# The RWKV stage of a bidirectional diffusion step: A of both directions first, block transfers on two queues, one stationary for the output side

## The chip, the core and the metric

The kernel runs on one core of a Trainium2 chip. The metric is the device time of one execution in microseconds (us), the median of several executions. The engines of the core that matter are the TensorE (PE in the profile: matmuls; PEld is its loading of stationary operands), the VectorE (DVE), the ScalarE (ACT), GpSimd (POOL) and the SyncE (SP), which here does nothing but issue DMAs. Each engine works through its instructions in the order of the program and waits at an instruction until what it needs is there; so a waiting instruction holds everything behind it on its engine, also the DMAs that are issued from that engine's queue.

## The reference

One step of a hybrid block over 640 tokens of width 2048 (512 latent tokens and 128 context tokens): a projection into eight parts, an RWKV-7 scan in both directions over 16 heads of 64 channels, an RG-LRU branch, a gated merge, and an output projection.

```python
def rwkv7_scan(r, w, k, v, kk, a, s0, reverse):
    def step(s, inp):
        r_t, w_t, k_t, v_t, kk_t, a_t = inp
        s_kk = jnp.einsum('bhvk,bhk->bhv', s, kk_t)
        s = s * w_t[:, :, None, :] - s_kk[..., None] * (kk_t * a_t)[:, :, None, :] + v_t[..., None] * k_t[:, :, None, :]
        return s, jnp.einsum('bhvk,bhk->bhv', s, r_t)
...
    z = xm @ p['w_in']
    r, k, v, g_a, x_b, g_b, m_a, m_b = jnp.split(z, SPLITS, axis=-1)
    r = r + (shift_fn(r) - r) * mu[0]
...
    for d in range(2):
        dirs_a.append(rwkv_direction(...))
```

The shift averages a token's neighbours: four on the grid for the latent tokens, two for the context tokens.

## The kernel before

**The background of matmuls.** All large products go through `product`, which runs over the K tiles of a product in steps (`piece`, L318): each step is six PE matmuls of 128x320 (L331). After each step `tick` (L229) lets the side work advance by one `yield`. So the program is one long row of steps, called **ticks** here, between which the side work's instructions are placed; how many ticks lie between two pieces of side work is written out in tuples (W, INV, QI, X1 and so on, L46 to L53). For every second tick one part of the next weights is split into a high half by ScalarE (`wh`, L313) and a low half by GpSimd (`wl`, L314), five parts (ten ticks) ahead of its use, into five buffers. Raw weights come by SP's queue (L301) into three buffers.

**The RWKV stage.** It goes over eight groups i of two heads (128 channels). Beside group i run seven products (`hosts`), 112 ticks; the first has nine and the seventh eight. Three generators work side by side: `mixed` shifts the r, k and v of group i+1 (`mix`, L755); `normed` (L885) prepares its decays and keys (`over` writes bk, the two key sides, L846); `rwkv` (L938) does the scan of group i in chunks of 64 tokens, ten chunks (NC) in two directions d and two heads e; then `norm` (L1219) closes group i.

**One scan, in ticks from its start.** `decayed` (L858) multiplies -kk and r by their decays into one tile st4. `first` (L951) multiplies each chunk's 64x64 key block with both halves of st4 (128 columns): its first half, masked, is A (`ats`), its second the r side (`rbs`). Six calls, three for each direction, ticks 2 to 14. `send` (L997) stores A's 32x32 diagonal blocks in DRAM; from there they come back with one block in a row (xn at L1069, xi at L1088), ScalarE turns them (L1092, L1095), and from tick 24 on VectorE inverts 80 triangular blocks at once by 30 steps of two operations (L1100, L1102). Between these steps lie `second` (L969: the other key side, again 128 columns, with VectorE's L982 bringing it in) and `turned` (L987: the keys transposed, `toks`). At tick 48 VectorE's copy L1109 has the inverses in both orders, four stores (L1113) take them to DRAM, at tick 53 four loads (tf, L1121) and eight loads (qm, L1127) bring them back; at tick 60 PE multiplies them with A's off-diagonal blocks (L1136, L1150) to get the inverse of the whole 64x64 block. From tick 64 on eight serial steps s (L1163) run through the chunks: `px` (L1169) and one half of the output `py` (L1173), a copy by ScalarE (L1176), `pu` (L1181), `put` into the tile sv (L1028 on ScalarE, L1029 on VectorE), then `pn` (L1190), the other half of `py` (L1194), and the new state (L1198, L1200). They end at tick 105. `ps1` gives one of four PSUM tiles in turn.

## Time and profile before

| | us |
|---|---|
| median of 3 executions | 2215.8 (2215.31 to 2216.61) |
| the profiled execution, its own time | 2214.5 |
| its span, first to last instruction | 2212.7 |
| scan of one group, from one L1136 to the next | 150.5 to 151.3 |
| one tick (six matmuls of L331) | 0.88 |

The granted TensorE clock is 0.981 on average. The profile gives busy times by engine, the waits with what ended them, and a timeline in which several equal instructions are merged into one row (start, length, engine, line, operation, shapes, count, and in brackets the idle time before it). A matmul's length in it overlaps the next one's; what a matmul costs is the distance of the starts.

### The profile page before, as it was taken

The page shows a single profiled execution, that of the slowest core. Times are in us where ns is not written, and L with a number is a line of the kernel's source. Part 1 is how long each engine was busy: PE and PEld are TensorE (multiplying, and loading weights), DVE is VectorE, ACT ScalarE, POOL GpSimd, SP SyncE. Part 2 cuts the span into 40 slices and gives each one's busy share as a digit, 9 for nine tenths or more (in the row PEclk, how much of TensorE's full clock was granted, in tenths as well). Part 3 has the DMA queues.
Part 4 walks back from the last instruction along what each step waited for, and adds up shares of the span by engine and source line. Part 5 has one row for each costly group of instructions (what it writes and reads, how often), then busy time and mean ns, then how long its engine had stood idle before and what let it go on. Part 6 is the DMA issues. An engine that isn't in the chain of part 4 may idle for free.

```text
span 2212.7 us, 47527 instructions
## 1 busy us (share of the span) xinstructions
PE 2106.8 (95%) x18248; PEld 1960.3 (89%) x18248; DVE 1371.9 (62%) x2661; ACT 973.4 (44%) x2262; POOL 882.9 (40%) x1167
## 2 busy tenths in 40 slices
PE   6999999999998998998989989989999899999997
PEld 3789999998888898898888988989989799999997
DVE  4755765687746756676676467665632699733354
ACT  3346776643443444434434434444333422234554
POOL 2244554553333333333333333334323465543343
PEclk9999999999999999999999999999999999999999
DMA  9953334332323222223223222232322767544474
GB/s 368 343 160 129 129 107 132 100 98 82 92 73 89 70 81 87 74 77 96 59 83 92 80 85 71 79 89 82 85 86 85 251 225 223 183 148 156 150 242 153
DMA packets 203507, 281.64 MB, mean 127 GB/s; under 512 B 69360, under 2 KB 91056, under 8 KB 202768
## 3 DMA queue, kind: packets, MB, share of 16 engines
q1 hardware_dynamic: 202832, 277.38, 39.8%
q8 instruction: 144, 2.36, 0.4%
q0 software_dynamic: 448, 1.23, 0.2%
q14 instruction: 83, 0.68, 0.1%
HBM read 237.70 MB, written 39.85 MB: 125 GB/s over the span
## 4 chain that ended last, share of the span: by engine, by line
PE 73%; DVE 16%; DMA 5%; issue 3%; ACT 1%; SPq 1%; POOL 0%; ACTq 0%; DVEq 0%; POOLq 0%
PE pj L331 55%; PE rw L591 3%; DVE tmp L1100 2%; DVE junk L1349 2%; DVE xi L1102 2%; PE rw L958 2%; PE rw L499 2%; DVE gws L1351 1%; PE pj L499 1%; PE rw L976 1%; PE rw L1181 1%; DVE st L982 1%; PE rw L1169 1%; DMA wr<-ws 1%; PE ada L385 1%
## 5 line engine op out<-in xcount | busy, mean ns | idle before, releaser
L314 POOL TENSOR_TENSOR wl<-wr,wh 128x256 fp32r<-128x256 f32 x922 | 792.5, 868 | 1230.1 <-ACT wh L313 1177.2
L331 PE MATMUL pj<-xh,wh 128*128 128x320 f32 (+2 forms) x2976 | 761.1, 323 | 1.4 <-ACT wh L313 1.4
L331 PE MATMUL pj<-xh,wl 128*128 128x320 f32 (+2 forms) x2976 | 724.8, 311 | 1.7 <-DVE wl L314 1.5
L331 PE MATMUL pj<-xl,wh 128*128 128x320 f32 (+2 forms) x2976 | 723.5, 310 | 0.0
L313 ACT ACTIVATE wh<-wr 128x256 fp32r<-128x256 f32 x1048 | 421.5, 413 | 512.4 <-PE pj L331 394.0
L331 PEld LDWEIGHTS pj<-xh,wh 128*128 128x128 f32 x2976 | 502.5, 190 | 33.6 <-issue 14.4
L331 PEld LDWEIGHTS pj<-xh,wl 128*128 128x128 f32 x2976 | 511.9, 189 | 4.1 <-DVE wl L314 2.5
L331 PEld LDWEIGHTS pj<-xl,wh 128*128 128x128 f32 x2976 | 512.8, 189 | 0.1
L1100 DVE TENSOR_TENSOR tmp<-xn,xi 104x30 f32<-104x30 f32 (+14 forms) x240 | 100.4, 418 | 81.0 <-ACT xn L1095 74.5
L1029 DVE COPY sv<-rw 64x128 f32<-64x128 f32 x80 | 23.6, 295 | 198.5 <-ACT sv L1028 197.3
L314 DVE TENSOR_TENSOR wl<-wr,wh 128x256 fp32r<-128x256 f32 x126 | 57.6, 458 | 127.2 <-ACT wh L313 127.1
L1102 DVE TENSOR_TENSOR xi<-xi,tmp 104x30 f32<-104x30 f32 (+14 forms) x240 | 98.7, 411 | 8.2
L1349 DVE SCALAR_TENSOR_TENSOR junk<-gws,cb 128x512 f32<-128x512 f32 x64 | 67.6, 1056 | 9.7 <-ACT cb L1341 9.7
L331 PE MATMUL pj<-yah,wh 128*128 128x320 f32 x256 | 59.3, 313 | 7.6 <-ACT g L1262 7.6
L982 DVE TENSOR_TENSOR st<-rw,c 64x512 f32<-64x512 f32 (+1 forms) x96 | 57.6, 600 | 12.4 <-PE rw L976 10.2
L1351 DVE SCALAR_TENSOR_TENSOR gws<-gws,cb 128x512 f32<-128x512 f32 x64 | 61.4, 959 | 1.9
L331 PE MATMUL pj<-yah,wl 128*128 128x320 f32 x256 | 59.3, 313 | 0.6 <-POOL wl L314 0.6
L331 PE MATMUL pj<-ybh,wh 128*128 128x320 f32 x256 | 58.6, 310 | 0.6 <-DVE thx L1385 0.4
L331 PE MATMUL pj<-yal,wh 128*128 128x320 f32 x256 | 59.1, 313 | 0.0
L331 PE MATMUL pj<-ybh,wl 128*128 128x320 f32 x256 | 58.6, 310 | 0.3 <-POOL wl L314 0.3
L331 PE MATMUL pj<-ybl,wh 128*128 128x320 f32 x256 | 58.3, 309 | 0.0
L1028 ACT ACTIVATE sv<-rw 64x128 f32<-64x128 f32 x80 | 21.7, 271 | 74.7 <-PE rw L1181 69.0
(776 smaller groups left out, 3088.0 us busy)
## 6 DMA issues: line engine op xcount, KB each, us to landing
wr<-w_in SPq DMA_DIRECT2D x312, 256.0 KB
adaw<-ada_w SPq DMA_DIRECT2D x64, 512.0 KB
wr<-w_o SPq DMA_DIRECT2D x128, 256.0 KB
gws<-ada_g SPq DMA_DIRECT2D x64, 256.0 KB
thl<-th SPq DMA_DIRECT2D x32, 320.0 KB
th<-thl SPq DMA_DIRECT2D x32, 320.0 KB
thm<-g SPq DMA_DIRECT2D x64, 160.0 KB
thx<-thm SPq DMA_DIRECT2D x32, 320.0 KB
```

The lines of the kernel that those rows point to most:

```text
L313: S.activation(h, r, AF.Copy)
L314: lows[pos[1] % len(lows)].tensor_tensor(lo, r, h.bitcast(F32), ALU.subtract)
L331: PE.matmul(p[:, :t1 - t0], w, x[:, t0:t1], start=(k == 0 and a == 0), stop=(k == nk - 1 and a == 2))
L499: PE.matmul(p[:, :HT], u[:, w], x[:, t], start=new, stop=end)
L591: PE.matmul(p, a, b, start=(n == 0), stop=(n == 2))
L958: PE.matmul(pa[hd(e), x:x + P], z.bk[d][hd(e), n, e], st4s[d][hd(e), n, e].rearrange("p a t -> p (a t)"), start=True, stop=True)
L982: V.tensor_tensor(st4s[d][so, n0:n0 + nn, e], pb[so, :m].rearrange("p (c a t) -> p c a t", a=2, t=CH), mb[so], ALU.mult)
L1029: V.tensor_copy(sv[hd(1), a, 1], src[hd(1), b])
L1100: V.tensor_tensor(t, xn[:NV, j, j + 1:].unsqueeze(2).to_broadcast([NV, m, j]), xi[:NV, j, :j].unsqueeze(1).to_broadcast([NV, m, j]), ALU.mult)
L1102: V.tensor_tensor(xi[:NV, j + 1:, :j], xi[:NV, j + 1:, :j], t, ALU.add)
L1349: V.scalar_tensor_tensor(junk, w, 1.0, cbs[h][:, 0], ALU.mult, ALU.mult, accum_out=gs[:, h, n, 0:1])
L1351: V.scalar_tensor_tensor(w, w, 1.0, cbs[h][:, 1], ALU.mult, ALU.mult, accum_out=gs[:, h, n, 1:2])
```

## The change

A of both directions now comes first. The r side is taken out of `first` and `second`: `decayed` is split into `inward` (-kk by its decay, into the tiles `sts`) and an `outward` of the scan's preparation (r by its decay, `z.rp`, done at the end of `normed`). `first` and `second` (now `across`) multiply 64 columns instead of 128, in two calls of five chunks for a direction instead of three. The r side is made by the new `outward(d, n0)`: both key sides together are one stationary operand of 64x128, so that one matmul gives both halves (`ros`). In the serial steps the output `py` comes after `pn` in one go: sv with `ros`, then the state `sc_` with `z.rp`. A lies in the bytes of `toks`, so `turned` moves behind the inverse, to ticks 63 and 64. Values and the bonus move behind `first`.

A of the backward direction goes to DRAM by ScalarE's queue, as do two of the four stores of the inverses and the four loads of `blocks(1)`, three ticks after the rest. VectorE, not ScalarE, turns the backward blocks. The tuples of ticks are new: the inverse starts at tick 15 and has 33 ticks (it was 24 and 23), the stores are at tick 49, PE's use of the inverses at tick 59, the serial steps go from tick 65 to 104. `mix` adds the neighbours with six VectorE operations straight into r, k or v, without a tile for the sum. The slots are 14 instead of 13.

```diff
-QB, NQ, HP, BC, BG = 21, 7, (4, 3, 3), 5, 2
-W = (2, 2, 2, 2, 2, 2, 2, 2, 2, 1, 3, 2)
-INV = (0, 1, 1, 1, 1, 1, 1, 1, 2, 2, 2, 2, 2, 2, 2, 2)
-QI = (1, 5, 7, 3, 1)
-X1 = (1, 2, 1, 1, 2, 1, 1, 1)
-X2 = (2, 2, 2, 2, 2, 1, 2, 2)
+QB, NQ, HP, BC, BG = 20, 6, (4, 3, 3), 4, 2
+LQA = 3
+W, SD, LD = (2, 1, 4), 0, (4, 6)
+MV, MX = (1, 2, 2), 3
+IW = (1, 3, 5, 7, 9)
+INV = (0, 1, 1, 2, 2, 3, 2, 3, 3, 2, 3, 3, 2, 2, 2, 2)
+QI = (1, 2, 8, 3, 1, 0, 1)
+X1 = (1, 2, 1, 1, 2, 0, 1, 1)
+X2 = (3, 2, 2, 1, 2, 1, 2, 1)
...
+NSLOT = 14
...
-                s = slot("sh")
-                sv = chunks(s)
-                V.tensor_tensor(sv[:, 0:8], zr[:, :, 0:64], zr[:, :, 2:66], ALU.add)
...
-                V.scalar_tensor_tensor(o[:, :TS], s[:, :TS], dc(3 + q, i), o[:, :TS], ALU.mult, ALU.add)
-                V.scalar_tensor_tensor(o[:, TS:T], s[:, TS:T], dc(6 + q, i), o[:, TS:T], ALU.mult, ALU.add)
+                ov, m4, m2 = chunks(o), dc(3 + q, i), dc(6 + q, i)
+                for x, y in ((ov[:, 0:8], zr[:, :, 0:64]), (ov[:, 0:8], zr[:, :, 2:66]), (ov[:, 1:8], zr[:, 0:7, 1:65]),
+                             (ov[:, 0:7], zr[:, 1:8, 1:65])):
+                    V.scalar_tensor_tensor(x, y, m4, x, ALU.mult, ALU.add)
+                    yield
+                for y in (zp[:, 0:128], zp[:, 2:130]):
+                    V.scalar_tensor_tensor(o[:, TS:T], y, m2, o[:, TS:T], ALU.mult, ALU.add)
...
+            def outward(self, d):
+
+                t = self.r if d else slot("rp")
+                V.tensor_tensor(chunks(t), chunks(self.r), self.pin[d], ALU.mult)
+                self.rp[d] = chunks(t)
...
+            def inward(self, d, st):
+
                 for e in range(2):
-                    sl = hd(e)
-                    V.tensor_tensor(self.st4[d][sl, n, e, 0], chunks(self.nk)[sl, n], self.pex[d][sl, n], ALU.mult)
-                    V.tensor_tensor(self.st4[d][sl, n, e, 1], chunks(self.r)[sl, n], self.pin[d][sl, n], ALU.mult)
+                    V.tensor_tensor(st[hd(e), :, e], chunks(self.nk)[hd(e)], self.pex[d][hd(e)], ALU.mult)
...
+            for d in range(2):
+                yield
+                z.outward(d)
+            z.th = z.kd = z.pin = z.k = z.r = None
...
-            st4s = z.st4 = [rp.tile([P, NC, 2, 2, CH], F32, tag=f"st4{d}", name="st4") for d in range(2)]
-            rbs = [rp.tile([P, NC, CH], F32, tag=f"rb{d}", name="rb") for d in range(2)]
+            sts = [rp.tile([P, NC, 2, CH], F32, tag=f"st{d}", name="st") for d in range(2)]
+            ros = [rp.tile([P, NC, 2, CH], F32, tag=f"ro{d}", name="ro") for d in range(2)]
...
-            ats = [None, None]
+
+            ats = [t[:, :, 0] for t in toks]
...
             def first(d, n0):
 
-                nn = min(4, NC - n0)
-                pa, m = ps1(), nn * P
-                for n in range(n0, n0 + nn):
-                    x = P * (n - n0)
-                    for e in range(2):
-                        PE.matmul(pa[hd(e), x:x + P], z.bk[d][hd(e), n, e],
-                                  st4s[d][hd(e), n, e].rearrange("p a t -> p (a t)"), start=True, stop=True)
+                pa = ps1()
+                for n, e, x in both(n0):
+                    PE.matmul(pa[hd(e), x], z.bk[d][hd(e), n, e], sts[d][hd(e), n, e], start=True, stop=True)
 
                 def bring():
-                    mb = mask[d].unsqueeze(1).to_broadcast([P, nn, 2, CH])
-                    pav = pa[:, :m].rearrange("p (c a t) -> p c a t", a=2, t=CH)
-                    V.tensor_tensor(chunks(ats[d])[:, n0:n0 + nn], pav[:, :, 0], mb[:, :, 0], ALU.mult)
-                    V.tensor_tensor(rbs[d][:, n0:n0 + nn], pav[:, :, 1], mb[:, :, 1], ALU.mult)
+                    V.tensor_tensor(ats[d][:, n0:n0 + 5], five(pa), wide(mask[d][:, 0]), ALU.mult)
...
-            def second(d, n0):
...
-                    x = P * (n - n0)
-                    for e in range(2):
-                        PE.matmul(pb[hd(1 - e), x:x + P], z.bk[d][hd(e), n, 1 - e],
-                                  st4s[d][hd(e), n, e].rearrange("p a t -> p (a t)"), start=True, stop=True)
...
+            def across(d, n0):
+
+                pk = ps1()
+                for n, e, x in both(n0):
+                    PE.matmul(pk[hd(1 - e), x], z.bk[d][hd(e), n, 1 - e], sts[d][hd(e), n, e], start=True, stop=True)
+                for e in range(2):
                     so = hd(1 - e)
-                    V.tensor_tensor(st4s[d][so, n0:n0 + nn, e],
-                                    pb[so, :m].rearrange("p (c a t) -> p c a t", a=2, t=CH), mb[so], ALU.mult)
-
-                return lambda: bring(0), lambda: bring(1)
+                    V.tensor_tensor(sts[d][so, n0:n0 + 5, e], five(pk)[so], wide(mask[d][:, 0])[so], ALU.mult)
+
+            def outward(d, n0):
+
+                po = [ps1(), ps1()]
+                for n, e, x in both(n0):
+                    PE.matmul(po[e][:, x], z.bk[d][hd(e), n].rearrange("p a t -> p (a t)"), z.rp[d][hd(e), n],
+                              start=True, stop=True)
+                for e in range(2):
+                    V.tensor_tensor(ros[d][:, n0:n0 + 5, e], five(po[e]), wide(mask[d][:, 1]), ALU.mult)
...
                         p0 = CH * e + HB * b
-                        nc.sync.dma_start(sa[d][0][2 * e + b].rearrange("n r c -> r n c"),
-                                          chunks(ats[d])[p0:p0 + HB, :, HB * b:HB * (b + 1)])
+                        (nc.sync, nc.scalar)[d].dma_start(sa[d][0][2 * e + b].rearrange("n r c -> r n c"),
+                                          ats[d][p0:p0 + HB, :, HB * b:HB * (b + 1)])
...
-            z.decayed(0, 0, 4)
...
-            values(0)
-            yield from idle(W[0])
...
+            def moved():
+
+                values(0, 4)
+                values(4, 8)
+                yield
+                values(8, NC)
+
+                pb = heads([z.bonus])
+                for s in range(2):
+                    h = slice(s * HT, (s + 1) * HT)
+                    V.tensor_tensor(v[:, h], v[:, h], pb[s][:, :HT], ALU.mult)
+                z.bonus = None
+                yield
+                for f in (across, outward):
+                    for d in range(2):
+                        for n0 in (0, 5):
+                            f(d, n0)
+                            yield
+
+            for d in range(2):
+                z.inward(d, sts[d])
             yield from idle(W[2])
-            bring()
-            bring = first(0, 8)
...
+            for d in range(2):
+                bring = first(d, 0), first(d, 5)
+                for f in bring:
+                    f()
+                later(SD, lambda d=d: send(d))
+
+                later(LD[d], lambda x=(xn[0:NB], xi[64:NV])[d], d=d: nc.sync.dma_start(
+                    x, sa[d][0].rearrange("g n r c -> (g n) r c")))
+                yield from idle(W[d])
+            z.nk = z.pex = None
             work = moved()
+            for n in MV:
+                next(work)
+                yield from idle(n)
+            S.activation(xi[0:NB], xn[0:NB].rearrange("p j t -> p t j"), AF.Copy)
             next(work)
-            yield from idle(W[7])
...
-            S.activation(xn[64:NV], xi[64:NV].rearrange("p t j -> p j t"), AF.Copy)
-            yield from idle(W[11])
+            yield from idle(MX)
+            V.tensor_copy(xn[64:NV], xi[64:NV].rearrange("p t j -> p j t"))
...
                 if j % 2 == 0:
-                    next(work, None)
+                    if j // 2 in IW:
+                        next(work)
                     yield from idle(INV[j // 2])
-            for _ in work:
-                pass
             V.memset(xi[:NV].rearrange("p t s -> p (t s)")[:, ::HB + 1], 1.0)
             V.tensor_copy(xn[:NV], xi[:NV].rearrange("p t s -> p s t"))
             yield from idle(QI[0])
-            for d in range(2):
-                for w, x in ((1, xi), (2, xn)):
-                    nc.sync.dma_start(sa[d][w].rearrange("g n r c -> (g n) r c"), x[64 * d:64 * d + NB])
-            yield from idle(QI[1])
+            for w, x in ((1, xi), (2, xn)):
+                for d in range(2):
+                    (nc.sync, nc.scalar)[w - 1].dma_start(sa[d][w].rearrange("g n r c -> (g n) r c"),
+                                                          x[64 * d:64 * d + NB])
+            for _ in work:
+                yield from idle(QI[1])
...
-            for o in (1, 0):
+            def blocks(o):
...
-                        nc.sync.dma_start(qm[d][p0, :, HB * b:HB * (b + 1)],
-                                          sa[d][2 - d][2 * e + b].rearrange("n r c -> r n c"))
+                        (nc.sync, nc.scalar)[o].dma_start(qm[d][p0, :, HB * b:HB * (b + 1)],
+                                                          sa[d][2 - d][2 * e + b].rearrange("n r c -> r n c"))
+
+            blocks(0)
+            later(LQA, lambda: blocks(1))
             put(0, 4, sc_)
...
             yield from idle(QI[4])
+            for n in range(4):
+                turned(n % 2, n // 2 * 5)
+                yield from idle(QI[5 + n % 2])
...
-                px, py = ps1(), ps1()
-                for x in range(np_):
...
-                for x in range(np_):
-                    for e in range(2):
-                        PE.matmul(py[hd(e), x * CH:(x + 1) * CH], sv[:, at(s, x), e], st4s[x % 2][:, ch[x], e, 1],
-                                  start=(x == 0), stop=False, skip_group_check=True)
+                xe = [(x, e, slice(x * CH, (x + 1) * CH)) for x in range(np_) for e in range(2)]
+                px = ps1()
+                for x, e, o in xe:
+                    PE.matmul(px[hd(e), o], sts[x % 2][:, ch[x], e], sv[:, at(s, x), e], start=True, stop=True)
...
                 if s < 7:
                     pn = ps1()
...
-                for x in range(np_):
-                    for e in range(2):
-                        PE.matmul(py[hd(e), x * CH:(x + 1) * CH], sv[hd(e), at(s, x), e], rbs[x % 2][hd(e), ch[x]],
-                                  start=False, stop=True, skip_group_check=True)
+                    for x, e, o in xe:
+                        PE.matmul(pn[hd(e), o], toks[x % 2][:, ch[x], e], sv[:, at(s, x), e], start=True, stop=True)
+                py = ps1()
+                for x, e, o in xe:
+                    PE.matmul(py[hd(e), o], sv[:, at(s, x), e], ros[x % 2][:, ch[x], e], start=(x == 0), stop=False,
+                              skip_group_check=True)
+                for x, e, o in xe:
+                    PE.matmul(py[hd(e), o], sc_[hd(e), x], z.rp[x % 2][hd(e), ch[x]], start=False, stop=True,
+                              skip_group_check=True)
```

More of the change, by code (lines that the diff above doesn't have):

```diff
@@ L734, in slot @@
         def slot(name, dtype=F32):
[L735 removed]
+            return rp.tile([P, SLOT], dtype, tag="rs", name=name, bufs=NSLOT)
         def mixed(q, i):
@@ L1033, in rwkv @@
             G.memset(sc_[:, 2:4], 0.0)
-            values(0)
-            yield from idle(W[0])
-            values(1)
-            bring = first(0, 0)
-            z.decayed(0, 4)
-            yield from idle(W[1])
-            ats[0] = slot("at")
-            bring()
-            bring = first(0, 4)
-            z.decayed(1, 0, 4)
-            yield from idle(W[2])
-            bring()
-            bring = first(0, 8)
-            z.decayed(1, 4)
-            yield from idle(W[3])
-            bring()
@@ L1051, in rwkv @@
-            z.pin = z.pex = None
-            later(2, lambda: send(0))
-            bring = first(1, 0)
-            yield from idle(W[4])
-            ats[1] = slot("at")
-            bring()
-            bring = first(1, 4)
-            pb = heads([z.bonus])
-            yield from idle(W[5])
-            bring()
-            bring = first(1, 8)
-            yield from idle(W[6])
-            bring()
-            for s in range(2):
-                h = slice(s * HT, (s + 1) * HT)
-                V.tensor_tensor(v[:, h], v[:, h], pb[s][:, :HT], ALU.mult)
@@ L1068, in rwkv @@
-            later(2, lambda: send(1))
-            later(2, lambda: nc.sync.dma_start(xn[0:NB], sa[0][0].rearrange("g n r c -> (g n) r c")))
-            def moved():
-                for d in range(2):
-                    for n0 in (0, 4, 8):
-                        for bring in second(d, n0):
-                            yield
-                            bring()
-                        if n0 < 8:
-                            yield
-                            turned(d, n0 // 4 * 5)
-                        yield
+            def moved():
[14 more added lines that the diff above has]
+                            yield
@@ L1093, in rwkv @@
-            yield from idle(W[10])
-            next(work)
-            S.activation(xn[64:NV], xi[64:NV].rearrange("p t j -> p j t"), AF.Copy)
-            yield from idle(W[11])
+            yield from idle(MX)
+            V.tensor_copy(xn[64:NV], xi[64:NV].rearrange("p t j -> p j t"))
             for j in range(1, HB - 1):
```

79 lines of the change are left out of this document (24 added, 55 removed).

## Prediction

> **What bounds the kernel now.** First the page: the busy times, and the chain that ended last by engine.
>
> ```profile
> PE 2106.8 (95%) x18248; PEld 1960.3 (89%) x18248; DVE 1371.9 (62%) x2661; ACT 973.4 (44%) x2262; POOL 882.9 (40%) x1167
> PE 73%; DVE 16%; DMA 5%; issue 3%; ACT 1%; SPq 1%; POOL 0%; ACTq 0%; DVEq 0%; POOLq 0%
> ```
>
> PE has work for 95% of the span, so a change pays where it takes matmuls away or ends a wait of PE. The change touches only the RWKV stage. Next, PE's waits there, from 440 to 1760 us (us in all, times, longest), and PE's timeline around one of them:
>
> ```profile
> PE rw L1136 <- DMA xi<-scr: 39.0, 12, 6.3
> ```
> ```profile
> 1011.24 2.08 PE L1136 MATMUL rw<-xi,at 32*32 32x32 f32 x80 [5.55 <-DMA xi<-scr]
> 1013.25 0.90 PE L331 MATMUL pj<-xh,wh 128*128 128x320 f32 x2
> ...
> 1016.45 0.45 PE L331 MATMUL pj<-xh,wh 128*128 128x320 f32 x2
> 1017.43 0.89 PE L1150 MATMUL rw<-qm,xn 32*32 32x32 f32 x80
> ```
>
> PE stands 39.0 us in all for the inverses to come back from DRAM, 5.55 us here. The price is higher than the gap, because PE runs slowly behind it: the 80 small matmuls of L1136 take 2.08 us and those of L1150 later 0.89, so 1.2 us are lost there; the twelve matmuls from 1013.25 to 1016.45, two ticks, take 3.20 us instead of 1.76, so 1.4 us more. One wait costs 5.55 + 2.6 us.
>
> Who is late? VectorE, in the inverse of the next group. PE's timeline, then VectorE's, and VectorE's work from 1118.4 to 1156.3 in groups by line (busy us, mean ns):
>
> ```profile
> 1115.39 1.09 PE L976 MATMUL rw<-st,bk 64*64 64x128 f32 x16
> ...
> 1162.33 0.74 PE L1136 MATMUL rw<-xi,at 32*32 32x32 f32 x6 [6.25 <-DMA xi<-scr]
> ```
> ```profile
> 1118.49 0.19 DVE L1100 TENSOR_TENSOR tmp<-xn,xi 104x30 f32<-104x30 f32 x1 [9.49 <-ACT xn L1095]
> ...
> 1155.15 1.09 DVE L1109 COPY xn<-xi 104x1024 f32<-104x1024 f32 x1
> ```
> ```profile
> L1100 DVE TENSOR_TENSOR tmp<-xn,xi 104x30 f32<-104x30 f32 (+14 forms) x30 | 13.2, 438 | 10.3 <-ACT xn L1095 9.5
> L1102 DVE TENSOR_TENSOR xi<-xi,tmp 104x30 f32<-104x30 f32 (+14 forms) x30 | 11.9, 397 | 1.0
> L982 DVE TENSOR_TENSOR st<-rw,c 64x512 f32<-64x512 f32 (+1 forms) x10 | 5.8, 582 | 0.3
> ```
>
> From the first step to the end of the copy (1155.15 + 1.09) VectorE needs 37.75 us: 25.1 for the inverse, 5.8 for L982, the rest the mixing of r, the copy and gaps. Another 6.1 us go by through DRAM until PE can start (1156.24 to 1162.33). PE meanwhile passes tick 24 at 1118.2 (1115.39, 1.0 for the 16 matmuls, two ticks) and stands at tick 60 at 1156.1 (1162.33 less 6.25): 37.9 us for 36 ticks. So 0.3 + 37.75 + 6.1 - 37.9 gives back the wait of 6.25 us.
>
> **The change part by part.** PE's own work first, by the distance of the starts:
>
> ```profile
> 1022.17 0.68 PE L1181 MATMUL rw<-xt__12636,qm 64*64 64x64 f32 x16
> 1022.78 0.56 PE L331 MATMUL pj<-xh,wh 128*128 128x320 f32 x2
> ...
> 1091.37 1.09 PE L958 MATMUL rw<-st,bk 64*64 64x128 f32 x16
> 1092.39 0.56 PE L331 MATMUL pj<-xh,wh 128*128 128x320 f32 x2
> ...
> 1094.35 0.65 PE L958 MATMUL rw<-st,bk 64*64 64x128 f32 x8
> 1094.93 0.56 PE L331 MATMUL pj<-xh,wh 128*128 128x320 f32 x2
> ...
> 1112.10 0.53 PE L992 MATMUL rw<-c,bk 64*128 64x64 f32 x10
> 1112.55 0.56 PE L331 MATMUL pj<-xh,wh 128*128 128x320 f32 x2
> ```
>
> Removed for each group: `first` and `second`, eight calls of 16 matmuls at 1.02 us and four of 8 at 0.58, 10.5 us. Added: `first` with 2 x 20 matmuls of the form of L1181 (0.61 for 16, so 0.038 each), 1.5 us; `across` with four calls of ten, 0.45 each, 1.8; `outward` with four calls of ten in the tile form of L992 (0.45), 1.8. That makes 5.1 us, and some 0.2 more because the ten transposes of the values fall into three calls. Saved: 5.2 us, over eight groups **42 us**. `outward` is a real product where L992 transposes, so its price is bounded: 0.038 a matmul as L1181, or 0.064 as the 128 column matmuls of L958, which would take back 0.7 us a group. I take 0.045, its own form. The serial steps keep their matmuls, and `turned` only moves.
>
> Now the wait. The new schedule gives from VectorE's turning copy (tick 15) to PE's use (tick 59) 44 ticks, 38.7 us, plus six calls at 0.45 and about 0.1 for changing over, 42.0 us: 4.1 more than the 37.9 of before, although PE's own work there shrank. VectorE's part: the turned copy is new on it (1.1 us, as the 1024 elements of L1109; bounded above by the 2.10 us that ScalarE takes for the same block, L1095 below); the ten L982 go (5.8) and four operations of `across` and six of `outward` come, of 320 elements each where L982 has 427 in the mean at 0.58 us: some 0.48, bounded above by 0.58, so 4.8 us. So 37.75 + 1.1 - 1.0 = 37.9 us. The six operations of `mix` handle as many elements as before; I cost them at nothing, and they lie in VectorE's row behind the inverse's steps, so an extra 0.3 us each would be 1.8 us more on the wait. Of the way through DRAM I expect 0.4 us less, since two of the four stores start on ScalarE's queue beside SP's (an issue takes some 0.46, by the row of L1001 below). The start counts like the 0.3 of before: A leaves at tick 7, backward blocks come at tick 12, and the load has three ticks and a call (3.1 us), which xn's load also had. Together 0.3 + 37.9 + 5.7 - 42.0 = 1.9 us of wait, bounded by 0 and, with a copy of 2.1 us, slower masked products (1 us) and slower mixing (1.8), by 6.
>
> What a short wait costs, besides itself, is read from two others in PE's timeline:
>
> ```profile
> 551.95 0.54 PE L882 MATMUL rw<-qhh,blk 128*128 128x320 f32 x1 [3.04 <-DVE st L982]
> ...
> 553.62 0.73 PE L331 MATMUL pj<-xl,wh 128*128 128x320 f32 x2
> ...
> 1052.49 0.45 PE L1169 MATMUL rw<-sv,st 128*64 128x64 f32 x8 [1.34 <-ACT sv L1028]
> ```
>
> After 3.04 us two matmuls of L331 are long (0.73; a pair at full rate has 0.45 in the row at 1016.45). After 1.34 us the eight small matmuls are not: 0.45, beside 0.68 for sixteen in the row of L1181. I let 1.9 us cost only itself: 8 x 1.9 = 15 us. The Trainium skill, "TensorE: Matmul & The Clock Gate", Part 1, has TensorE fall to half its clock after an idle window of about 3.4 us, free running; by that rule a wait of 1.9 us would as a rule stay free of the 2.6 us. The trace agrees on the half rate, and shows it after 3.04 us already.
>
> Away go the waits of before: 39.0, with 2.6 for each of the seven groups that show one, 18, and in the first group the 3.04 us above with some 2 of slow matmuls (PE waits there for a PSUM tile that a late L982 holds; `outward` frees its tiles long before): **62 us**.
>
> New waits. In the serial steps `py` no longer lies between `px` and `pu`; one step has no tick at all between them (X1[5] is 0), so PE waits for ScalarE's copy (bounded above by 0.39 us, half the row of L995 below, which has 320 elements instead of 128) and two handovers, some 0.7 us. ScalarE gets `turned`'s eight copies (0.77 a pair) right behind the copies of the inverse, before the first `pu`: 3.1 us of work in a place that was free of it; I put 1.2 us on PE. Ten DMAs are issued from ScalarE; the trace of before has none there, SP's are the nearest (two lines of the source, with least, median and most ns of an issue), and rows of ScalarE's timeline:
>
> ```profile
> L1001 SPq DMA_DIRECT2D scr<-at x64: 357/459/620, 501.8 to 1574.8; - x64
> L1127 SPq DMA_DIRECT2D qm<-scr x64: 403/458/1911, 563.5 to 1630.0; - x64
> ```
> ```profile
> 1112.66 0.77 ACT L995 ACTIVATE tok<-rw 128x320 f32<-128x320 f32 x2 [2.03 <-PE rw L992]
> ...
> 1116.37 2.10 ACT L1095 ACTIVATE xn<-xi 40x1024 f32<-40x1024 f32 x1
> ...
> 1160.31 0.74 ACT L892 ACTIVATE q<-nk 128x640 f32<-128x640 f32 x1 [11.53 <-DVE nk L890]
> ```
>
> At 0.46 us that is 4.6 us of ScalarE a group, of which it saves 2.1 with L1095. What counts is the waiting: the two stores stand on ScalarE at tick 49 until VectorE's copy is done, some 6 us, and `blocks(1)` at tick 54 until the stores have landed. Behind them stand the `wh` parts. PE has up to ten ticks, 8.8 us, of parts in hand, and the last row shows ScalarE already held for 11.5 us at that place before. So nothing more than the 1.9 us above: 8 x (0.7 + 1.2) = **15 us**, bounded by 0 and by the second rival.
>
> Against ScalarE's queue speaks the Trainium skill, "Trainium Kernel Development and Optimization", Key Constraints: DMAs issued from SP, ScalarE and GpSimd run on the same 16 DMA engines, and a second issuer only saves issue time. By it the moved stores bring the 0.4 us above and no faster transfer, and the sum stays.
>
> Sum, against the profiled execution's own 2214.5 us: 2214.5 - 42 - 62 + 15 + 15 = 2140.5; the median shown is 1.3 above it, so **2142 us**.
>
> **The rivals.** First, **the wait stays**: the work taken from PE between ticks 15 and 59 is given back, because VectorE and DRAM set the end. For it: VectorE is busy almost without a gap through the inverse, and 1.9 us is a small difference of large numbers. Against it: nine more ticks. At 6 us and 2.6 us a group: 2214.5 - 42 - 62 + 8 x 8.6 + 15 = 2194, with the median's 1.3 about 2195.
>
> Second, **ScalarE's queue starves PE**, which is the slower side. If an issue there costs what the longest on SP cost (1.91 us), the two stores and `blocks(1)` hold ScalarE for 6 + 3.8 + 4 + 7.6 = 21 us around ticks 49 to 58, with hardly a `wh` between; beyond the 8.8 us of parts in hand PE stands still some 12.2 us and then runs slowly for 2.6, every group: 2214.5 - 42 - 62 + 8 x 14.8 = 2229, 2230 as a median. The savings are 104 us, 13 a group, so it decides from 8.8 + 13 - 2.6 = 19 us of ScalarE held. For it: a wait on that queue holds everything behind it; against it: SP's usual 0.46.
>
> Third, **everything is hidden**: VectorE's start is earlier, no wait is left, ScalarE keeps up. 2214.5 - 42 - 62 = 2110.5, about 2112.
>
> **How the numbers follow.** The forecast has 0.50 (its own range 2122 to 2162), the wait that stays 0.25, all hidden 0.15, starving 0.10. The range reaches from the third case, a little below it for `outward` at L1181's price, to the first: 2107 to 2195. It leaves out the starving case and little else. A measurement of this kernel can tell about 0.2% from no change; faster 0.89, same 0.02, slower 0.09.
>
> **What would show it.** In the profile of the changed kernel: `outward`'s ten matmuls at 0.45 us (start to start), `first`'s twenty at some 0.75; the period from one pz to the next near 141 us; L1136 waiting 1 to 3 us with full-rate matmuls behind it; ScalarE's rows with a hole from tick 49 of 6 us, and PE's L331 without waits for `wh`. The prediction is wrong if VectorE's stretch from the turned copy to the end of the copy that L1109 was is over 40 us, if L331 waits for `wh` or `wl`, or if `pu` waits more than 1 us in several steps.

## The result and the profile after

The changed kernel takes 2183.5 us (median of 4, 2182.12 to 2184.33) beside 2216.2 for the kernel before in the same runs: a ratio of 0.985 (95% interval 0.9833 to 0.9867). The forecast was 2142. The sign is right and the time lies in the range, but of the 74 us foretold 33 came. The profiled execution took 2183.02 us, its span is 2181.2.

The busy times of the changed kernel, and PE's waits from 440 to 1760 us (us in all, times, longest):

```profile
PE 2096.7 (96%) x18888; PEld 1965.7 (90%) x18888; DVE 1373.3 (63%) x2557; ACT 964.6 (44%) x2254; POOL 890.4 (41%) x1167
```
```profile
PE rw L1172 <- DVE sv L1034: 9.5, 5, 1.9
...
PE rw L975 <- DVE st L867: 7.1, 2, 6.7
PE rw L881 <- DVE v L1050: 4.6, 8, 0.6
PE rw L1159 <- ACT sv L1033: 3.7, 7, 1.4
PE rw L1123 <- DMA xi<-scr: 2.3, 5, 0.9
```

Two things are to be seen. The wait for the inverses, 39.0 us before, is 2.3 (L1123 is the old L1136). And PE has not fewer matmul rows but more: 18888 for 18248, where the forecast took half of the cost of the products with bk away.

PE's timeline with one call each of `first` (both halves, L975), `across` (L986) and `outward` (L995), and the L335 behind each, whose start ends its cost:

```profile
1078.72 1.38 PE L975 MATMUL rw<-st,bk 64*64 64x64 f32 x40
1080.03 0.56 PE L335 MATMUL pj<-xh,wh 128*128 128x320 f32 x2
...
1090.05 0.80 PE L986 MATMUL rw<-st,bk 64*64 64x64 f32 x20
1090.78 0.56 PE L335 MATMUL pj<-xh,wh 128*128 128x320 f32 x2
...
1103.43 1.33 PE L995 MATMUL rw<-rp,bk 64*128 64x64 f32 x20
1104.69 0.56 PE L335 MATMUL pj<-xh,wh 128*128 128x320 f32 x2
```

The code issues ten products in a call of `across` (five chunks, two heads), the profile counts 20 (the x20; each counted matmul is called a row below); the old `first` issued eight and its count was 16. So a product of these fp32 tiles is **two rows** of the profile, while a transpose is one (the ten of L992 were x10). The 640 rows that PE has more fit: a group had 160 rows of products with bk and has 240 now, eighty more in each of eight groups. Two calls of `first` cost 1.31 us, a call of `across` 0.73, a call of `outward` 1.26 (1103.43 to 1104.69), not 0.75, 0.45 and 0.45.

Where one group's time went, from one pz to the next, by the distance of the starts in PE's timeline (before 1011.24 to 1162.33, after 996.12 to 1142.72):

| us of PE in one group | before | after |
|---|---|---|
| background matmuls (L331, L335), the slow ones behind waits with them | 108.46 | 107.73 |
| wait ahead of the next pz | 6.25 | 0 |
| pz itself (L1136, L1123) | 2.01 | 1.36 |
| products with bk (L958, L976; then L975, L986, L995) | 10.51 | 10.58 |
| serial steps, their matmuls | 15.98 | 16.51 |
| transposes, head sums, second pz | 6.54 | 6.70 |
| other waits | 1.34 | 3.72 |
| sum | 151.09 | 146.60 |

Over all seven periods from the first pz to the last the time fell from 1061.0 us to 1031.6.

Without its 42 us the prediction's own sum is 2214.5 - 62 + 30 = 2182.5, almost the time measured. That is luck: its smaller errors, taken up below, nearly cancel.

### The profile page after: what moved, and what is told of

The parts are those of the page before. It is cut to its first block, busy times and chain, and to the rows that moved or that the text cites. A ratio compares the mean times of both kernels' runs of the same rounds, so it can differ in the third digit from the quotient of the medians.

```text
span 2181.2 us, 48631 instructions
## 1 busy us (share of the span) xinstructions
PE 2096.7 (96%) x18888; PEld 1965.7 (90%) x18888; DVE 1373.3 (63%) x2557; ACT 964.6 (44%) x2254; POOL 890.4 (41%) x1167
## 4 chain that ended last, share of the span: by engine, by line
PE 74%; DVE 15%; DMA 4%; issue 2%; ACT 2%; POOL 1%; SPq 0%; ACTq 0%; DVEq 0%; POOLq 0%
PE pj L335 56%; PE rw L595 3%; DVE junk L1333 2%; PE rw L503 2%; DVE tmp L1083 2%; DVE gws L1335 1%; PE pj L503 1%; PE rw L995 1%; DVE xi L1085 1%; DMA wr<-ws 1%; PE rw L1159 1%; PE rw L1165 1%; PE ada L389 1%; PE rw L1178 1%; PE rw L975 1%
## 5 line engine op out<-in xcount | busy, mean ns | idle before, releaser
L335 PE MATMUL pj<-xh,wh 128*128 128x320 f32 (+2 forms) x2976 | 756.9, 322 | 1.8 <-ACT wh L317 1.8
L335 PE MATMUL pj<-xh,wl 128*128 128x320 f32 (+2 forms) x2976 | 723.3, 310 | 1.7 <-DVE wl L318 1.5
L335 PE MATMUL pj<-xl,wh 128*128 128x320 f32 (+2 forms) x2976 | 722.5, 310 | 0.0
L335 PEld LDWEIGHTS pj<-xh,wh 128*128 128x128 f32 x2976 | 501.3, 189 | 23.0 <-ACT wh L317 2.4
L335 PEld LDWEIGHTS pj<-xh,wl 128*128 128x128 f32 x2976 | 511.1, 189 | 3.3 <-DVE wl L318 2.5
L335 PEld LDWEIGHTS pj<-xl,wh 128*128 128x128 f32 x2976 | 512.3, 189 | 0.1
L1083 DVE TENSOR_TENSOR tmp<-xn,xi 104x30 f32<-104x30 f32 (+14 forms) x240 | 109.4, 456 | 7.2 <-ACT g L1246 0.4
L335 PE MATMUL pj<-yah,wh 128*128 128x320 f32 x256 | 59.1, 312 | 7.7 <-ACT g L1246 7.7
L335 PE MATMUL pj<-yah,wl 128*128 128x320 f32 x256 | 59.1, 312 | 0.5 <-POOL wl L318 0.5
L335 PE MATMUL pj<-ybh,wh 128*128 128x320 f32 x256 | 58.6, 310 | 0.4 <-DVE thx L1369 0.4
L335 PE MATMUL pj<-yal,wh 128*128 128x320 f32 x256 | 58.8, 311 | 0.0
L335 PE MATMUL pj<-ybh,wl 128*128 128x320 f32 x256 | 58.4, 309 | 0.3 <-POOL wl L318 0.3
L335 PE MATMUL pj<-ybl,wh 128*128 128x320 f32 x256 | 58.3, 309 | 0.0
L335 PEld LDWEIGHTS pj<-yah,wh 128*128 128x128 f32 x256 | 43.4, 190 | 7.9 <-ACT g L1246 7.9
```

Source lines behind the costliest of these rows:

```text
L335: PE.matmul(p[:, :t1 - t0], w, x[:, t0:t1], start=(k == 0 and a == 0), stop=(k == nk - 1 and a == 2))
L1083: V.tensor_tensor(t, xn[:NV, j, j + 1:].unsqueeze(2).to_broadcast([NV, m, j]), xi[:NV, j, :j].unsqueeze(1).to_broadcast([NV, m, j]), ALU.mult)
```

## The experiments

Each was timed beside the kernel before, and the ratios are to that kernel. It took between 2215.6 and 2219.4 us in these sittings, so differences of some 4 us between the changed kernel and a variant say nothing. Three questions stood open: whether PE's work really stayed the same (theory A) or shrank and was given back (B), what the removed wait was worth, and what the change's other parts (ScalarE's queue, the one stationary, the mixing) brought.

**What a call of `outward` costs.**

```diff
-                for n, e, x in both(n0):
+                for n, e, x in [*both(n0), *both(n0)]:
                     PE.matmul(po[e][:, x], z.bk[d][hd(e), n]...
```

> The changed kernel with every product of outward issued twice into the same PSUM tile; nothing else differs. Theory A (PE's work did not shrink, because a product of these tiles stands in the profile as two rows, and a call of outward takes 1.26 us and not 0.45): four calls a group, eight groups, 32 x 1.26 = 40 us more than the changed kernel's 2183.5, so 2222 us, ratio to the kernel before 1.003. Theory B (the prediction's price was right, 0.45 a call, and the saving was given back in waits elsewhere): 32 x 0.45 = 14 us more, 2198, ratio 0.992.

Measured: 2217.7 us, ratio 1.001 (1.0001 to 1.0019), 34.2 more than the changed kernel: 1.07 us for each of the 32 calls. The wait for the inverses could hide no more than its 2.3 us. PE's timeline of this kernel:

```profile
1121.78 2.45 PE L995 MATMUL rw<-rp,bk 64*128 64x64 f32 x40
1124.16 0.56 PE L335 MATMUL pj<-xh,wh 128*128 128x320 f32 x2
```

Twenty products are 40 rows and cost 2.38 us. Theory A holds; 0.45 a call is refuted.

**Whether the gain was the wait alone: the kernel before with more cover.**

```diff
-QI = (1, 5, 7, 3, 1)
+QI = (1, 5, 13, 3, 1)
```

> The kernel before with six more ticks between the block loads and pz (QI[2] 7 to 13); nothing else of the change. Theory A (the whole gain of the change is the wait for the inverses, which only wanted cover): 6 ticks are 5.3 us against waits of 5.5 to 6.3, so less than 1 us of wait stays; of 39 us of waits and 18 of slow matmuls behind them some 50 go, 2166 us, ratio 0.977, faster than the changed kernel. Theory B (the six ticks only make the group longer, the lateness returns at its end or in the next group's start): 2205 to 2225, ratio 0.995 to 1.004.

Measured: 2242.4 us, 1.0108 (1.0091 to 1.0126). Neither theory foresaw a loss. PE's waits, ScalarE's timeline and PE's:

```profile
PE pj L331 <- ACT wh L313: 31.1, 6, 6.0
```
```profile
708.99 0.74 ACT L892 ACTIVATE q<-nk 128x640 f32<-128x640 f32 x1 [13.29 <-DVE nk L890]
```
```profile
710.09 0.90 PE L331 MATMUL pj<-xh,wh 128*128 128x320 f32 x2 [5.79 <-ACT wh L313]
```

The wait for the inverses is gone, but ScalarE's square of nk waits 13.29 us for VectorE, which works off the inverse first, and no `wh` is made behind it. PE, which had stood at pz, now runs on into the end of its parts in hand. The hold is there in the kernel before too (11.53 us in the prediction's row), but PE stands at pz meanwhile and uses no parts. It is the mechanism of the prediction's second rival, on the other kernel and by another instruction.

**The same, with the inverse started earlier.**

```diff
-W = (2, 2, 2, 2, 2, 2, 2, 2, 2, 1, 3, 2)
+W = (2, 1, 1, 1, 1, 1, 1, 2, 2, 1, 3, 2)
-QI = (1, 5, 7, 3, 1)
+QI = (1, 5, 13, 3, 1)
```

> The kernel before with the products of A six ticks closer together at the group's start (W[1] to W[6] 2 to 1) and those six ticks put between the block loads and pz (QI[2] 7 to 13): the inverse starts six ticks earlier and pz stays where it is. None of the change's products, queues or copies. Theory A (the change's gain is the earlier start of the inverse alone; its products cost PE what the old ones did): of 6.3 us of wait less than 1 stays, and ScalarE's hold for nk shrinks with it, so 30 to 55 us less than before, 2160 to 2186, ratio 0.975 to 0.987. Theory B (the new products carry the gain, or the closer ticks make PE wait for the masked copies at the start): 2200 to 2216, ratio over 0.993.

Measured: 2246.0 us, 1.0125 (1.0109 to 1.0141): slower, a miss for both. PE's waits:

```profile
PE rw L1136 <- DMA xi<-scr: 17.9, 14, 3.8
PE rw L976 <- DVE st L982: 13.7, 6, 3.1
```

Half of the wait stays and a new one is there: `second` wants PSUM tiles that VectorE empties by L982 between the steps of the inverse. Neither of these two ways of moving ticks frees the old schedule. Whether the new products or only their new order made it work was not separated further.

**What the wait is worth in the changed kernel.** Six ticks of cover go behind pz:

```diff
-QI = (1, 2, 8, 3, 1, 0, 1)
+QI = (1, 2, 2, 9, 1, 0, 1)
```

> The changed kernel with six of the ticks ahead of pz put behind it (QI[2] 8 to 2, QI[3] 3 to 9); all else at the same tick. The inverses come about 2.3 us before pz now (8.4 us from the end of VectorE's copy to pz where the kernel before took 6.1), so 6 x 0.88 - 2.3 = 3 us of wait a group. If a wait costs itself and the slow matmuls behind it (the prediction's 2.6 us, here at least the 1.2 us of pz itself): 8 x 4.2 to 5.6 = 34 to 45 us more, 2217 to 2228, ratio 1.001 to 1.006. If the time of the wait is won back, since VectorE and not PE sets the pace behind it: 2190 to 2205, ratio under 0.995.

Measured: 2229.2 us, 1.0045 (1.003 to 1.006), 45.7 more than with the cover: the first of the two cases. VectorE's copy of the inverses, and PE's timeline behind it:

```profile
1156.28 1.07 DVE L1091 COPY xn<-xi 104x1024 f32<-104x1024 f32 x1
```
```profile
1163.99 1.71 PE L1123 MATMUL rw<-xi,tok 32*32 32x32 f32 x80 [3.46 <-DMA xi<-scr]
1165.63 0.90 PE L335 MATMUL pj<-xh,wh 128*128 128x320 f32 x2
1166.33 0.73 PE L335 MATMUL pj<-xl,wh 128*128 128x320 f32 x2
1166.87 0.73 PE L335 MATMUL pj<-xh,wl 128*128 128x320 f32 x2
1167.40 0.67 PE L335 MATMUL pj<-xh,wh 128*128 128x320 f32 x2
1167.91 0.45 PE L335 MATMUL pj<-xl,wh 128*128 128x320 f32 x2
```

The wait of 3.46 us costs 5.4 in this group: itself, 0.8 in pz (1.64 us from start to start, where pz takes 0.82 when nothing holds it), and 1.1 in the eight background matmuls behind (2.28 us for 1.17 at full rate). Eight groups at 45.7 / 8 = 5.7 agree with that. It is the prediction's way of pricing a wait, shown. From the copy's end (1157.35) to pz pass 6.6 us.

Shorter waits can cost the same. In the last group PE stands 1.21 us ahead of pz and 0.55 more inside it, and the matmuls from 1631.92 to 1635.50 run slowly all the same:

```profile
1629.12 0.57 PE L1123 MATMUL rw<-xi,tok 32*32 32x32 f32 x4 [1.21 <-DMA xi<-scr]
...
1632.30 0.73 PE L335 MATMUL pj<-xh,wh 128*128 128x320 f32 x2
```

So the prediction's choice to let 1.9 us cost only itself does not hold in general, although the idle window of about 3.4 us that it took from the Trainium skill, "TensorE: Matmul & The Clock Gate", Part 1, speaks for it; here the measurement decides. The changed kernel itself doesn't test it, as its longest wait ahead of pz is 0.9 us.

**ScalarE's queue.** All stores and block loads by SP:

```diff
-                        (nc.sync, nc.scalar)[d].dma_start(sa[d][0]...
+                        nc.sync.dma_start(sa[d][0]...
```

and so for the stores of xn and for `blocks(1)`.

> The changed kernel with all its stores and block loads on SP's queue again (A of the second direction, the two stores of xn, the four loads of the other blocks), at the same ticks. Theory A (ScalarE's queue saves issue time only): four stores and loads more on SP in a row at 0.46 us make the inverses come back 1 to 2 us later; the changed kernel waits there 0.3 us a group, so 0 to 1.5 us a group, 2183 to 2195, ratio 0.985 to 0.990. Theory C (ScalarE's queue is what took the wait away): 3 us and more of wait a group with slow matmuls behind it, over 2207, ratio over 0.996.

Measured: 2179.6 us, 0.9838 (0.9825 to 0.9852). The interval overlaps that of the change: the queue brings nothing that can be seen. The rule that the prediction cited, the Trainium skill, "Trainium Kernel Development and Optimization", Key Constraints (a second issuer only saves issue time), agrees with this.

**Two more ticks in the serial steps.**

```diff
-X1 = (1, 2, 1, 1, 2, 0, 1, 1)
-X2 = (3, 2, 2, 1, 2, 1, 2, 1)
+X1 = (1, 2, 1, 1, 2, 1, 1, 1)
+X2 = (3, 2, 2, 2, 2, 1, 2, 1)
```

> The changed kernel with one tick more at two places of the serial steps: after pu of the fourth step (X2[3] 1 to 2) and after px of the sixth (X1[5] 0 to 1). Theory A (the new waits there, 9.5 us for sv in five groups and 8 x 0.44 for xt, are for want of a tick, and ticks are to be had): 9.5 + 3.5 = 13 us less, 2171, ratio 0.979. Rival: the wait moves on to the next step, since VectorE is behind with other work, and the group only ends two ticks later: 2180 to 2186, ratio 0.984 to 0.987.

Measured: 2186.5 us, 0.987 (0.9854 to 0.9887): the rival, and not to be told from the changed kernel. VectorE's timeline of this kernel ahead of the copy that PE's fourth step waits for:

```profile
1039.73 1.03 DVE L816 TENSOR_SCALAR th<-th 128x640 f32<-128x640 f32 x1
1040.80 1.90 DVE L818 TENSOR_TENSOR_SCAN th<-smask,th 128x640 f32<-128x640 bf16 x1
1042.62 1.97 DVE L770 SCALAR_TENSOR_TENSOR v<-z,dv,v 128x512 f32<-128x512 f32 x2
1044.62 0.29 DVE L1034 COPY sv<-rw 64x128 f32<-64x128 f32 x1
```

The copy stands behind 4.9 us of a scan and of the mixing of v. The wait for sv grew to 13.1 us in 11 places; the tick was given to PE, but the queue ahead of the copy is VectorE's.

**The mixing as before**, first alone, which takes three ticks where the new form takes four, and then with an empty tick (one more `yield`) behind it:

```diff
-                for x, y in ((ov[:, 0:8], zr[:, :, 0:64]), ...
-                    V.scalar_tensor_tensor(x, y, m4, x, ALU.mult, ALU.add)
+                V.tensor_tensor(sv[:, 0:8], zr[:, :, 0:64], zr[:, :, 2:66], ALU.add)
```

> The changed kernel with the mixing of the neighbours as before (three sums and two products into a tile of its own, in three ticks, instead of six products into the result in four). Theory A (the new form costs VectorE more, 4.2 us against 3.3 a mixing by its rows, but VectorE's stretch no longer sets PE's end, since the wait for the inverses is 0.3 us a group): within 4 us of the changed kernel, 2180 to 2187. Theory D (three mixings a group lie on VectorE ahead of a copy that PE waits for, v's ahead of the fourth step's sv): 0.9 to 1.9 us a group come back, 2168 to 2176, ratio 0.978 to 0.982.

> The changed kernel with the mixing as before, and one empty tick behind it so that a mixing takes as many ticks as the new form. Theory A (the 24 us of the old mixing alone came from the tick that it is shorter: ScalarE's square of nk then stands ahead of the four block loads on ScalarE's queue, waits 3.6 us for VectorE, and PE waits 2 us a group for qm): the wait of PE for qm goes, 2180 to 2190, ratio 0.983 to 0.988. Theory D (the old form itself costs, by its own tile or its sums): 2200 to 2210, ratio over 0.991.

Measured: 2207.9 us, 0.9946 (0.993 to 0.9962), without the tick; 2174.8 us, 0.9803 (0.9786 to 0.9819), with it. All four numbers missed: the first is slower than both of its theories, the second faster. The first one's ScalarE and PE:

```profile
1008.70 0.74 ACT L899 ACTIVATE q<-nk 128x640 f32<-128x640 f32 x1 [3.55 <-DVE nk L897]
1009.35 0.40 ACT L317 ACTIVATE wh<-wr 128x256 fp32r<-128x256 f32 x1
1010.38 2.14 ACTq L1115 DMA_DIRECT2D qm<-scr  x4
```
```profile
1017.25 0.83 PE L1141 MATMUL rw<-qm,xn 32*32 32x32 f32 x74 [2.03 <-DMA qm<-scr]
```

and the changed kernel's ScalarE at that place:

```profile
990.86 3.09 ACTq L1111 DMA_DIRECT2D qm<-scr  x4
994.55 0.74 ACT L895 ACTIVATE q<-nk 128x640 f32<-128x640 f32 x1 [3.41 <-DMA qm<-scr]
```

One tick less in the mixing puts the square of nk ahead of the four loads on ScalarE; it waits for VectorE, the loads start late, and PE stands for qm in eight places, 10.6 us in all. With the tick the loads come first again, and PE has no such wait:

```profile
986.28 3.10 ACTq L1116 DMA_DIRECT2D qm<-scr  x4
989.59 0.74 ACT L900 ACTIVATE q<-nk 128x640 f32<-128x640 f32 x1 [2.99 <-DMA qm<-scr]
```

So theory A's reason for the 24 us is right. With the order restored the old form is 9 us faster than the new one. Why is only partly seen: over the seven periods the background matmuls take 4.0 us less, and pz with the wait ahead of it 2.9 less. The wait for sv, theory D's place, is 9.8 us in the stage for 9.5. VectorE's work for a mixing is about equal (62.5 us for 16 mixings, 67.6 for 16.5).

**The one stationary.** Each 64x128 product as two of 64x64, the two heads on the diagonal of TensorE's 128x128 array and then across it, so that each product uses one quadrant:

```diff
-                for n, e, x in both(n0):
-                    PE.matmul(po[e][:, x], z.bk[d][hd(e), n].rearrange("p a t -> p (a t)"), z.rp[d][hd(e), n],
-                              start=True, stop=True)
+                for n in range(n0, n0 + 5):
+                    x = slice(CH * (n - n0), CH * (n - n0 + 1))
+                    for a in range(2):
+                        for e in range(2):
+                            h = a ^ e
+                            PE.matmul(po[e][hd(h), x], z.bk[d][hd(e), n, h], z.rp[d][hd(e), n], start=True, stop=True)
```

> The changed kernel with each product of outward (one 64x128 stationary) as two with 64x64 stationaries into the two halves of the same tile, the heads' products side by side on the diagonal and then across it. Theory A (a 64x128 product costs as much as the two it stands for, since two heads' 64x64 products run beside each other and two 64x128 ones do not): twice the rows of first and across, 2.62 + 2.92 = 5.5 us a group for 5.04, so 0 to 4 us more, 2183 to 2188, ratio 0.985 to 0.987. Theory B (one stationary halves the cost): 5 us a group more, 40 us, 2223, ratio 1.003.

Measured: 2170.9 us, 0.9785 (0.9768 to 0.9802), 12.6 faster than the change; both theories missed. PE's timeline:

```profile
1084.33 0.80 PE L986 MATMUL rw<-st,bk 64*64 64x64 f32 x20
...
1097.71 0.81 PE L999 MATMUL rw<-rp,bk 64*64 64x64 f32 x40
1098.45 0.56 PE L335 MATMUL pj<-xh,wh 128*128 128x320 f32 x2
```

Forty rows in four quadrants cost 0.74 us; twenty in two quadrants (L986) 0.73; twenty with the 64x128 stationary 1.26. The Trainium skill, "TensorEngine Tiling (Array Packing)", Key Properties, says that tiles of the array run matmuls in parallel: the trace agrees for four of 64x64. For the 64x128 products no such gain is seen, at 0.126 us each beside 0.037 for a 64x64 product in four quadrants; no run has one head's alone, so whether two of them overlap at all stays open.

**Four quadrants for `first` and `across`.** Both in one loop, with their masked copies behind each call, one call a tick; this takes one tick more, and a second version takes one tick out again ahead of the copies of A:

```diff
-W, SD, LD = (2, 1, 4), 0, (4, 6)
+W, SD, LD = (1, 1, 4), 0, (4, 6)
...
-IW = (1, 3, 5, 7, 9)
+IW = (3,)
...
+                    for a in range(2):
+                        for e in range(2):
+                            h = a ^ e
+                            PE.matmul(po[a][hd(h), x], z.bk[d][hd(e), n, h], sts[d][hd(e), n, e], start=True, stop=True)
```

and in the second version

```diff
-MV, MX = (1, 2, 2), 3
+MV, MX = (1, 2, 1), 3
```

> The kernel with two stationaries for outward, and first and across in one loop: a head's product on the diagonal of TensorE's array is followed by the same head's product across it, so that four quadrants have work, into two PSUM tiles; one call a tick, its masked copies right behind it. A group gets one tick more and across leaves VectorE's stretch of the inverse. Theory A (PE's time in these products is set by how many quadrants of the array have a product at once: 160 rows in four quadrants took 2.96 us a group, 80 in two took 2.62): first and across together 2.96 instead of 2.62 + 2.92, 2.58 us a group or 20 us less than the 2171 of two stationaries, 2150, ratio 0.969. Rival (PE waits for the masked copies at the group's start or for the inverse, whose cover shrinks by the same 2.6 us): 2165 to 2180, ratio 0.976 to 0.983.

> The kernel with first and across in one loop over four quadrants, and one tick taken out again ahead of the copies of A (MV's last 2 to 1), so that all from there on stands at the tick of the changed kernel. Theory A (the 38 us by which the longer version missed 2150 came from that tick, which put ScalarE's square of nk ahead of the four block loads): PE's wait for qm goes, 2150 to 2160, ratio 0.969 to 0.974. Rival (the cover that PE's shorter work takes away is missing, the wait for the inverses comes back): 2170 to 2185.

Measured: 2188.1 us, 0.9864 (0.9842 to 0.9885), and in step 2170.9 us, 0.9786 (0.9765 to 0.9807). The products did get cheaper, 3.28 us a group in the second version for the 5.54 of `first` and `across`, as one call of forty rows shows there:

```profile
1075.25 0.81 PE L979 MATMUL rw<-st,bk 64*64 64x64 f32 x40
1075.99 0.56 PE L335 MATMUL pj<-xh,wh 128*128 128x320 f32 x2
```

But PE's waits of the two versions are:

```profile
PE rw L1134 <- DMA qm<-scr: 8.9, 8, 2.1
```
```profile
PE rw L1120 <- DMA xi<-scr: 9.8, 14, 2.7
```

The first has the order of the old mixing's case again, and lies above both numbers. The second is level with the two stationaries alone (2170.9): it has lost a part of the cover of the inverses, and its rival holds. All on SP's queue with the extra tick still in:

> The kernel with first and across in one loop, and all stores and block loads on SP's queue. Theory A (ScalarE's queue is worth nothing here, as in the changed kernel, where SP's queue alone gave 2179.6 for 2183.5): 2146 to 2152, within 4 us of the same kernel with both queues. Theory C (with less of PE's work between the inverse and pz, the four stores and loads more on one queue show): 1 to 2 us a group more, 2158 to 2166.

Measured: 2186.3 us, 0.9853 (0.9834 to 0.9872): as slow as with both queues, which is theory A's difference, though 34 us above its number. PE's wait for qm is 18.7 us here; the loads of `th` stand on SP's queue between the first four loads of qm and the other four.

**Adding up.** The four quadrants in step with the old mixing, the same with two ticks more ahead of pz, the two stationaries with the old mixing, and that with SP's queue alone. The two ticks are:

```diff
-QI = (1, 2, 8, 3, 1, 0, 1)
+QI = (1, 2, 10, 3, 1, 0, 1)
```

> The same with the mixing as before in four ticks. If the savings add up (9 us for the old mixing, from 2183.5 to 2174.8): 2141 to 2151, ratio 0.965 to 0.970. If VectorE's lateness is what both of them cut, it is saved once: 2150 to 2160, no better than without.

> The kernel with four quadrants for first and across and with the mixing as before, and two ticks more ahead of pz (QI[2] 8 to 10), behind all stores, loads and the square of nk in program order. Theory A (the shorter work of PE uncovered the inverses, whose wait took most of the saving back): two ticks are 1.8 us a group, the wait of 8.1 us in the stage goes with the slow matmuls behind it, 10 to 16 us less than the 2161.7 without them, 2146 to 2152, ratio 0.967 to 0.970. Rival (the group ends two ticks later and something else is late then): 2158 to 2166, ratio 0.972 to 0.976.

> The changed kernel with two 64x64 stationaries for outward and the mixing as before in four ticks, first and across apart as in the change. If the savings add up (12.6 and 8.7 us): 2162, ratio 0.975. If PE waits for something else instead: 2168 to 2175.

> The changed kernel with two stationaries for outward, the mixing as before in four ticks, and all stores and block loads on SP's queue: of the change, A first with its inverse nine ticks earlier is left. Theory A (ScalarE's queue is worth nothing): 2158 to 2165, ratio 0.974 to 0.977, that of the two undone. Theory C (with a shorter VectorE stretch and a shorter PE stretch, the queue shows): 2170 and more, ratio over 0.979.

Measured: 2161.7 us, 0.9737 (0.9712 to 0.9763); 2186.7 us, 0.9862 (0.9845 to 0.9878); 2164.2 us, 0.976 (0.9741 to 0.978); 2166.1 us, 0.9771 (0.9753 to 0.9789). The first, the third and the fourth beat both kernels and can't be told from each other. The savings add up as far as can be seen: the old mixing takes 9.2 us from the four quadrants in step (2170.9), clear of both intervals, and 6.7 from the two stationaries, where the intervals still touch. The first misses its number because the four quadrants had missed theirs. The fourth is theory A again: without ScalarE's queue nothing is lost. The two ticks were a miss: the wait for the inverses went, and other waits came, with ticks and VectorE's work now differently placed to each other. PE's waits there:

```profile
PE rw L1161 <- ACT sv L1036: 8.8, 6, 1.7
...
PE rw L1006 <- ACT tok L1008: 6.8, 12, 1.4
PE rw L984 <- DVE st L989: 6.8, 16, 0.8
```

## Why the prediction was off

**The step that failed is "PE's own work", 42 us.** It counted the products of the new calls in the code (ten, twenty) and priced them with rows of the profile, in which the old calls' eight products counted 16; for `across` and `outward` it took the price of ten transposes, which are one row each. Measured: 10.51 us a group before, 10.58 after, so nothing saved. The bound it gave, 0.064 a matmul, is what a row of `outward` costs; but there were 20 rows and not ten. With the rows counted, the prediction's own prices would have given 80 rows each of `first` and `across` at 0.038 and 80 of `outward` at 0.064, 11.2 us a group for the 10.5 taken out: no saving. Halving the columns halved the cost of `first` and `across` (1.31 us for ten products of 128 columns in both, and 0.65 to 0.73 for ten of 64); the r side, taken out of them, then cost in `outward` what they had saved. The case for this is the doubled `outward` (+34.2 us) and the two stationaries (-12.6): PE's work is on the path, and its price goes by rows and by how they lie on the array.

**The waits of before, 62 us, went** about as priced. Over the seven periods PE's wait ahead of pz fell from 38.8 us to 2.3, pz itself from 12.9 to 8.1, and the background matmuls from 768.0 to 758.8, 50.5 us together; the prediction's 39 and 18 less the wait that it left make 42. In the first group the wait of 3.04 us went, but the one for the decayed keys grew by 3.6 (7.1 us in all at L975, 3.5 before). That a wait is worth more than itself was shown by the cover taken away.

**The residual wait, 15 us, came out at 2.3.** VectorE's stretch was 38.8 us for the 37.9 foretold, and the way through DRAM 6.6 for 5.7 (read where the cover was taken away), so 45.7 with the start; but PE's passage was 47.2 for 42.0, since the six calls in it cost 6.5 us and not 2.7, and changes of shape and ticks did the rest. The two starts:

```profile
948.93 1.10 DVE L1079 COPY xn<-xi 40x1024 f32<-40x1024 f32 x1 [0.94 <-DMA xi<-scr]
```
```profile
996.12 1.42 PE L1123 MATMUL rw<-xi,tok 32*32 32x32 f32 x80
```

By this sum the work that PE hadn't lost was the cover. A little wait hides in that row: pz takes 1.36 us from start to start and not 0.82, since its first products still come one load at a time; over the seven periods that is 2.3 us more. The first rival, "the wait stays", is refuted for the change as made and came true in part (9.8 us) in the version with cheaper products.

**The new waits, 15 us, came out right in size,** 1.9 us a group as foretold (all of PE's waits but those ahead of pz, 10.3 us before and 23.8 after over the seven periods), but by luck, since they lie in other places. The step without a tick cost 0.44 a group (0.7 foretold), the crowded ScalarE behind the inverse some 0.4 (1.2); the largest, 1.89 us in five of the groups, is VectorE's copy of sv behind the mixing of v and a scan, where the change has one tick and the prediction priced nothing:

```profile
1037.65 0.39 PE L1172 MATMUL rw<-sv,tok 128*64 128x64 f32 x5 [1.89 <-DVE sv L1034]
```

The matmuls of the serial steps, costed as unchanged, take 5.7 us more over the seven periods; why isn't known.

**The mixing, costed at nothing,** costs 9 us by the version with the old form in step, some 1.1 a group. That is inside the prediction's bound of 1.8 on the wait for the inverses, but VectorE's stretch is the same in both (38.8 and 38.9 us in one group), so the place was wrong.

**ScalarE's queue:** the 0.4 us of a shorter way didn't show (6.6 us for 6.1), and the second rival, starving, didn't come: L335 waits 1.8 us for `wh` in all. Of the three signs by which the prediction was to be wrong none appeared clearly (L335 waits 2.1 us for `wh` and `wl`, 1.7 before): they look for a late engine or a wait, and the failure lay in PE's own work, where `outward`'s 1.26 us for the 0.45 showed it. The loads on that queue did show another risk, which the prediction hadn't named: an instruction ahead of them that waits for VectorE.

## What to carry over

Before pricing a new matmul by a line of the profile, count the products that the code issues for a line that is already there: here every fp32 product was two rows. Small products cost here by how many quadrants of the array had work at once, so issue them in turn over all four; the one wider stationary was dearer than the two it replaced. Where one engine's long stretch sets several dates (here the inverses, nk and sv), a tick won at one of them is lost at the next, and one tick more or less can change which instruction stands ahead in a queue.

## What the hardware showed unexpectedly

Ten fp32 products of 64x64 by 64 columns cost 0.73 us in two quadrants, and twenty cost 0.74 in four; ten of 64x128 cost 1.26 us. Ten fp32 transposes of the same tile form are ten rows where ten products are twenty. And after a wait of 3.46 us eight background matmuls took nearly twice their time (2.28 us for 1.17); matmuls ran as slowly after 1.8 us of standing (1.21 ahead of pz and 0.55 inside it).
